# Retention's gate tiles of three heads as block products in the first feed-forward's buffers, with v made one head ahead

## The chip, the core and the metric

The kernel runs on one core of a Trainium2 chip. A core has five engines with queues of their own: TensorE (PE in the profile, its weight loads PEld) multiplies matrices into PSUM; VectorE (DVE), ScalarE (ACT) and GpSimd (POOL) work elementwise; SyncE (SP) mostly issues DMA transfers. Transfers are also issued from ACT's and POOL's queues. The metric is the device time of one launch in microseconds (us), less is better. The kernel before takes 1470.64 us (median of three runs, 1469.88 to 1470.76).

## What is computed

A decoder step of two layers over 544 tokens: 512 of one new sequence, and 32 of eight sample groups of four. All data are float32.

```
x += short_conv(rmsnorm(x));  x += swiglu(rmsnorm(x))        # layer 0
x += retention(rmsnorm(x));   x += swiglu(rmsnorm(x))        # layer 1
return rmsnorm(x), and the new states

retention:  z = x @ w_in                      # (544, 1024) @ (1024, 6144)
            q, k, v, g = split(z)             # 1024, 1024, 2048, 2048 columns; 4 heads
            q, k = rotary(q), rotary(k) / 16
            o = decayed (q k^T) v + q S       # in chunks, per head: dk = 256, dv = 512
            out = (silu(g) * groupnorm(o) * gn_g) @ w_out
swiglu:     (silu(x @ w_gate) * (x @ w_up)) @ w_down        # 2816 hidden
```

The sample groups carry a state S of 256 x 512 for each group and head (1 MB for each of four pieces of a head), which is read, used, updated and written back.

## The kernel before, in words

**Products in two parts.** Every float32 operand is split into a high part (`xh`, `wh`, fp32r) and a low part (`xl`, `wl`), and a product is three: high by high, high by low, low by high. `split` makes the high part with a copy on ACT and the low part with a subtraction on DVE. `split_adding` leaves DVE out: ACT copies twice (the second time negated), and a transfer from POOL's queue adds the original on top. `load_piece` loads a weight piece of 512 KB with SP into one of three buffers `w` of the pool `wts`, and splits it into `wh`, `wl` (three each).

**Tiles.** Activations lie with features on the 128 partitions and the 544 tokens in the free direction, as two halves of 272. `project` multiplies one tile of 128 output features: 8 steps of the contraction x 3 products x 2 halves, 48 products of 272 columns (line 172). PSUM has eight banks: four single ones (`bank`, "sm" in the profile) and two pairs ("mm"), given out by `psum`.

**Feed-forward.** `ffn` takes two output tiles, each cut in two halves of tokens and two of the contraction, as a 2 x 2 block product, and makes it with seven block products in place of eight. `operands` makes the seven combinations of the activation's blocks once (tiles `oh`, `ol`, from a work tile `f` with two buffers); `weights7` makes the seven combinations of a pair of weight tiles. A `Job` is one such pair: 7 block products x 4 steps x 3 = 84 products of 272 columns (line 458). `run` goes through a list of jobs, and prepares the next one's weights while one multiplies. `summed` brings the block products together: snapshots by ACT, additions by DVE, in a tile `gu` (four buffers). The pools of a feed-forward are opened in this order: `ff` (gu), `ffp` (f), `sw` (weights' sums), `ffo` (oh, ol).

**Retention.** After the first feed-forward its pools close and three others open in the same memory: `rt` (most tiles, among them `gt` with the decay tables, `rot0`/`rot1` with the rotated q and k, `gate`, `rt0`, `rt1`, `yn`), `rt1` (small constants and `xs`, the normed sample tokens), `st` (three buffers for pieces of S). `qk_first` makes k and the first half of q for head 0, `qk_project` the other half. Then, for each head:

1. `value`: v for all 512 tokens in four banks (line 906 to 908, 24 products of 512 columns for each of four weight pieces) and for the sample tokens (line 913, which reads the unsplit weights, so `w` stays taken until then). After the second piece come the splits of q and k, the sample scores and the transposed keys.
2. `gate_project` 0, `sample_operands`, `state` 0, `gate_project` 1, `state` 1: two of the head's four gate tiles, and the recurrent state.
3. `scores`, then `gate_project` 2 and 3.
4. `sample_outputs` and `states_update` on the four pieces of S, the outputs `inner`, the normalization, the gating, and in between the next head's k and q (`qk_project`).
5. `out_project`: eight tiles that are added to x.

The last head has gate tiles 2 and 3 inside step 4.

**What sets the order.** The program is written as one list. The framework orders each engine's queue before the run, from a cost estimate of its own: among the instructions whose inputs it reckons ready, the one written first goes first; `issue_after` fixes an order by hand. Waits between engines come from the use of tiles: a tile's buffer is given out again when its last reader is done, and a pool's memory goes to a later pool when the earlier pools in it are closed.

Lines that the change and the steps below speak of:

Of the kernel before, what the change touches and what calls it, by code (L numbers as in the profile page):

```python
# [7 lines left out]
F32 = mybir.dt.float32  # L8
F32R = mybir.dt.float32r
AF = mybir.ActivationFunctionType  # L10
ALU = mybir.AluOpType
# [24 lines left out]
WARM = 8  # L36

# [9 lines left out]
def hybrid_decode_kernel(ctx: ExitStack, tc: tile.TileContext, a: dict, o: dict):  # L47
# [476 lines left out]
    def ffn(layer, next_gain):  # L524
        with ExitStack() as c1:
# [4 lines left out]
            oh = [one.tile([P, 7, HT], F32R, tag=f"oh{i}", name=nm("oh")) for i in range(KP)]  # L530
            ol = [one.tile([P, 7, HT], F32R, tag=f"ol{i}", name=nm("ol")) for i in range(KP)]
# [13 lines left out]

            def operand(k):
                f = fp.tile([P, 5, HT], F32, tag="f", name=nm("f"))
                for i in range(2):
                    nc.vector.scalar_tensor_tensor(
                        f[:, 2 * i : 2 * i + 2, :], halves(x[k + i * KP]), g_ffn(layer, k + i * KP), R,  # L550
                        op0=ALU.mult, op1=ALU.mult,
                    )
                operands(f, oh[k], ol[k])

            def whole_pairs():
# [4 lines left out]
                for m in range(WHOLE):  # L560
# [31 lines left out]
                    for k in range(2 * m, KP if m == WHOLE - 1 else 2 * m + 2):  # L592
                        operand(k)
# [101 lines left out]
            if layer == 1:  # L695
                final(last, group_acts(last), group_weights, fp, tp)

# [83 lines left out]
    ffn(0, lambda kt: g_mix(1, kt))  # L781


    with ExitStack() as c2:
# [23 lines left out]
        for kt in range(KT):  # L808
            nc.vector.tensor_scalar_mul(xs[:, kt, :], x[kt][:, SEQ:], g_mix(1, kt))
# [26 lines left out]
        def qk_first(st):  # L836

            steps = rms_scale(True, [bank(), bank()])
            ws = [load_piece(a["rtqk"][0, 2 + dt], KT * P) for dt in range(2)]
            pts = [psum() for _ in ws]  # L840
            for part in (MADE[:KP], MADE[KP:]):
                for (wh, wl), pt in zip(ws, pts):
                    first = part[0] == MADE[0]
                    project(pt, wh, wl, 0, xh, xl, first, not first, ks=part, weave=iter(()) if first else steps)
            qw, qpt = load_piece(a["rtqk"][0, 0], KT * P), [bank(), bank()]
            project(qpt, *qw, 0, xh, xl, weave=steps)
            drain(steps)
            for i, t in enumerate((cos, sin)):
                nc.sync.dma_start(t, a["rope"][i])
# [21 lines left out]
        def qk_rotate(st, which, dt, pt):  # L871
# [4 lines left out]
            if dt == 0:  # L876
                return
# [484 lines left out]
```

## Time and profile before

| | |
|---|---|
| median of three runs | 1470.64 us (1469.88 to 1470.76) |
| the profiled execution | 1470.36 us, span 1468.5 |
| PE busy | 1457.3 us, 99% |
| DVE, ACT, POOL busy | 920.5, 572.4, 84.3 us |
| moved by DMA | 172.83 MB, mean 118 GB/s |
| granted clock of PE | 0.999 |
| first feed-forward | ends at 574 us on PE |
| retention, head 0's first own product | 574 us |
| retention ends, second feed-forward begins | about 1083 us |
| transfer of a 512 KB weight piece, issue to landing | 3.5 to 4.1 us (median by source) |
| transfer of a 1 MB piece of S, in and out | 7.9 and 4.9 us |

How to read it: a share is of the span. An engine is busy while one of its instructions runs; the DMA share is the mean busy share of 16 DMA engines. "a <- b" in a wait means that a waited until b was done. The chain that ended last is followed back from the last instruction to what released it, step by step.

### The profile page before, as it was taken

How to read it: one execution, taken by the hardware profiler on the slowest of the kernel's cores; microseconds unless marked ns; L12 is line 12 of the kernel's file. 1: busy time of each engine (PE TensorE's matmuls, PEld its weight loads, DVE VectorE, ACT ScalarE, POOL GpSimd, SP SyncE). 2: the span in 40 equal slices, each digit the busy share in tenths (PEclk: the TensorE clock that was granted, in tenths of full speed). 3: DMA queues.
4: the chain of work that ended last, by engine and by line, in shares of the span. 5: the costliest groups of instructions: out<-in, count | busy, mean ns of one | idle time of the engine just before them, and what ended most of it. 6: DMA issues, size and time to landing. Idle time of an engine off the chain costs nothing.

```text
span 1468.5 us, 26015 instructions
## 1 busy us (share of the span) xinstructions
PE 1457.3 (99%) x11016; PEld 1388.8 (95%) x11016; DVE 920.5 (63%) x1397; ACT 572.4 (39%) x821; POOL 84.3 (6%) x107
## 2 busy tenths in 40 slices
PE   9999999999999999999999999999999999999998
PEld 9999999999999999897987988898799999999997
DVE  6545439847748647648645934844759847748645
ACT  5222355625525434242142224114265625525424
POOL 0100220000000003000000000000030000000002
PEclk9999999999999999999999999999999999999999
DMA  6222274232322325336335613714564232332322
GB/s 226 86 87 87 89 179 109 91 100 90 102 94 87 101 65 181 116 115 232 100 115 173 202 49 121 264 42 143 173 158 108 91 105 87 104 92 93 101 65 83
DMA packets 69748, 172.83 MB, mean 118 GB/s; under 512 B 6512, under 2 KB 23792, under 8 KB 69632
## 3 DMA queue, kind: packets, MB, share of 16 engines
q1 hardware_dynamic: 66576, 162.01, 33.9%
q0 software_dynamic: 2192, 7.94, 3.3%
q8 instruction: 86, 1.41, 0.4%
q10 hardware_dynamic: 864, 1.22, 0.2%
q14 instruction: 30, 0.25, 0.1%
HBM read 149.97 MB, written 21.18 MB: 117 GB/s over the span
## 4 chain that ended last, share of the span: by engine, by line
PE 93%; DVE 4%; DMA 2%; POOL 1%; ACT 0%; issue 0%; DVEq 0%; POOLq 0%; ACTq 0%; SPq 0%
PE mm L172 41%; PE sm L458 26%; PE sm L172 13%; PE sm L906 2%; PE sm L907 2%; PE sm L908 2%; DMA S<-in_rets_dram 2%; DVE S L1138 1%; PE sm L160 1%; PE sm L162 1%; PE sm L161 1%; PE sm L1117 1%; PE mm L913 1%; DVE yn L1048 0%; DVE wl L186 0%
## 5 line engine op out<-in xcount | busy, mean ns | idle before, releaser
L185 ACT ACTIVATE wh<-w 128x1024 fp32r<-128x1024 f32 (+4 forms) x215 | 210.0, 980 | 448.2 <-PE mm L172 252.2
L186 DVE TENSOR_TENSOR wl<-w,wh 128x1024 fp32r<-128x1024 f32 (+4 forms) x215 | 243.1, 1134 | 44.3 <-ACT wh L185 40.9
L172 PE MATMUL mm<-xh,wh 128*128 128x272 f32 x1060 | 222.7, 291 | 0.0
L172 PE MATMUL mm<-xh,wl 128*128 128x272 f32 x1060 | 219.2, 289 | 0.0
L172 PE MATMUL mm<-xl,wh 128*128 128x272 f32 x1060 | 218.8, 288 | 0.0
L172 PEld LDWEIGHTS mm<-xh,wh 128*128 128x128 f32 x1060 | 166.5, 189 | 5.0 <-DVE wl L186 3.4
L458 PE MATMUL sm<-oh,wh 128*128 128x272 f32 x576 | 166.7, 289 | 0.0
L458 PE MATMUL sm<-oh,wl 128*128 128x272 f32 x576 | 166.6, 289 | 0.0
L172 PEld LDWEIGHTS mm<-xl,wh 128*128 128x128 f32 x1060 | 166.4, 189 | 0.0
L458 PE MATMUL sm<-ol,wh 128*128 128x272 f32 x576 | 166.3, 289 | 0.0
L172 PEld LDWEIGHTS mm<-xh,wl 128*128 128x128 f32 x1060 | 165.5, 189 | 0.4
L266 DVE TENSOR_TENSOR x<-x,mm 128x544 f32<-128x544 f32 x85 | 61.2, 720 | 144.8 <-PE mm L172 144.8
L458 PE MATMUL sm<-oh,l 128*128 128x272 f32 x432 | 124.9, 289 | 0.0
L458 PE MATMUL sm<-oh,h 128*128 128x272 f32 x432 | 124.8, 289 | 0.0
L458 PE MATMUL sm<-ol,h 128*128 128x272 f32 x432 | 124.8, 289 | 0.0
L458 PEld LDWEIGHTS sm<-oh,wh 128*128 128x128 f32 x576 | 108.7, 189 | 0.5 <-ACT u L515 0.4
L458 PEld LDWEIGHTS sm<-oh,wl 128*128 128x128 f32 x576 | 108.8, 189 | 0.0
L458 PEld LDWEIGHTS sm<-ol,wh 128*128 128x128 f32 x576 | 108.6, 188 | 0.0
L186 DVE TENSOR_TENSOR l<-w,h 128x1024 fp32r<-128x1024 f32 x72 | 68.8, 956 | 55.6 <-ACT h L185 55.4
L172 PE MATMUL mm<-xh,f 128*128 128x272 f32 x576 | 99.3, 288 | 0.0
L172 PE MATMUL sm<-xh,wh 128*128 128x272 f32 x412 | 88.4, 291 | 0.3 <-DVE rs L219 0.3
L172 PE MATMUL sm<-xh,wl 128*128 128x272 f32 x412 | 86.7, 288 | 0.0
(268 smaller groups left out, 2866.5 us busy)
## 6 DMA issues: line engine op xcount, KB each, us to landing
w<-in_ffgu_dram SPq DMA_DIRECT2D x88, 512.0 KB, 3.5
w<-in_ffdn_dram SPq DMA_DIRECT2D x96, 192.0 KB, 2.5
S<-in_rets_dram SPq DMA_DIRECT2D x16, 1024.0 KB, 7.9
out_rets_dram<-S SPq DMA_DIRECT2D x16, 1024.0 KB, 4.9
w<-in_cvin_dram SPq DMA_DIRECT2D x21, 512.0 KB, 3.5
w<-in_rtqk_dram SPq DMA_DIRECT2D x16, 512.0 KB, 3.8
w<-in_rtv_dram SPq DMA_DIRECT2D x16, 512.0 KB, 3.9
w<-in_rtg_dram SPq DMA_DIRECT2D x16, 512.0 KB, 4.1
```

The costliest lines, as they stand in the source:

```text
L160: nc.tensor.matmul(out, lh, rh, start=start, stop=False, skip_group_check=True)
L161: nc.tensor.matmul(out, lh, rl, start=False, stop=False, skip_group_check=True)
L162: last_product[0] = nc.tensor.matmul(out, ll, rh, start=False, stop=stop, skip_group_check=True)
L172: last_product[0] = nc.tensor.matmul(half(pt, hf)[:, :HT], w[:, c], act[k][:, hf * HT : (hf + 1) * HT], start=(first and k == ks[0] and i ...
L185: h = nc.scalar.activation(dh, src, AF.Copy)
L186: nc.vector.tensor_sub(dl, src, dh.bitcast(F32))
L266: last_residual[0] = nc.vector.tensor_add(xk, xk, p)
L458: nc.tensor.matmul(out, w[:, c], b[k][:, at, :], start=(first and k == 0 and i == 0), stop=(k == n - 1 and i == 2), skip_group_check=True,)
L906: nc.tensor.matmul(out, xh[kt][:, ts_], wh[:, cw], start=(kt == 0), stop=False)
L907: nc.tensor.matmul(out, xh[kt][:, ts_], wl[:, cw], start=False, stop=False)
L908: nc.tensor.matmul(out, xl[kt][:, ts_], wh[:, cw], start=False, stop=(kt == KT - 1))
L913: nc.tensor.matmul(pvs[g * NS : (g + 1) * NS, 0, :], xs[:, kt, :], raw[kt // 2][:, kt % 2 * DV : (kt % 2 + 1) * DV], start=(c == 1), stop= ...
```

## The change

The gate tiles of heads 0, 1 and 2 (twelve of sixteen) leave retention. A new function `ahead` runs at the end of the first feed-forward, before its pools close. It makes k, q and v of head 0 and writes them, unrotated, to DRAM; makes the seven operands of the second layer's normed x in the feed-forward's `oh`, `ol`; and runs six jobs, one for each pair of gate tiles, whose results are passed through SiLU, scaled and written to DRAM by transfers from ACT's queue. The last job also loads the first two pieces of head 1's value weights.

Retention then loads: k and q of head 0 (`qk_loaded`, which scales and rotates them), v of the head at hand (`value_loaded`, through the buffer of the `gate` tile), and the finished gate tiles (into that same buffer afterwards). `value` becomes `value_products`, `value_out`, `value_sample` and `operands_made`: in head h the products of head h+1's v run, and its rows go through free buffers to DRAM (`value_out`, stored from ACT's queue). The states' loads are written inside the value products. The last head has no value products any more, and keeps its four gate tiles as they were.

The diff, cut to its core (the products inside `value_products` are those of `value`):

```diff
--- before.py
+++ after.py
+AHEAD = 3
...
+    def operand_tiles(one):
+        return [[one.tile([P, 7, HT], F32R, tag=f"{t}{i}", name=nm(t)) for i in range(KP)] for t in ("oh", "ol")]
+    def operand(k, fp, oh, ol, gain):
+        f = fp.tile([P, 5, HT], F32, tag="f", name=nm("f"))
+        for i in range(2):
+            nc.vector.scalar_tensor_tensor(
+                f[:, 2 * i : 2 * i + 2, :], halves(x[k + i * KP]), gain(k + i * KP), R, op0=ALU.mult, op1=ALU.mult,
+            )
+        operands(f, oh[k], ol[k])
+    def ffn(layer, next_gain, then=None):
...
+            if then is not None:
+                then(tp, fp, sw, one)
...
+    dram = ctx.enter_context(tc.tile_pool(name="dram", bufs=1, space=bass.MemoryType.DRAM))
+    qk_made = [dram.tile([P, 2, T], F32, tag=f"qk{w}", name=nm("qkm")) for w in range(2)]
+    v_made = [dram.tile([P, 5, DV], F32, tag=f"v{h}", name=nm("vm")) for h in range(NH)]
+    gate_made = [dram.tile([P, 4, T], F32, tag=f"g{h}", name=nm("gm")) for h in range(AHEAD)]
+    def value_piece(h, c, raw, adding=False):
+        return load_piece(a["rtv"][h, c], 2 * DV, keep=raw, adding=adding)
+    def value_products(h, xs, first=None, then=None, ws=None):
+        pv = [bank() for _ in range(4)]
+        pvs = psum()
+        if ws is None:
+            raw = []
+            ws = [value_piece(h, c, raw, first is None) for c in range(2)]
+        else:
+            ws, raw = ws
+        if first is not None:
+            first()
+        for c in range(4):
...
+            if c < 2:
+                ws.append(value_piece(h, c + 2, raw, first is None))
+            if then is not None:
+                then(c)
+        return pv, pvs
+    def value_out(h, pv, pvs, places):
+        for tt, (row, _) in enumerate(places):
+            nc.scalar.activation(
+                row, pv[tt] if tt < 4 else pvs[:, 0, :], AF.Copy, scale=rN[:, tt : tt + 1] if tt < 4 else rN[:, 5:6]
+            )
+            if places[tt][1] is not None:
+                at, src = places[tt][1]
+                nc.scalar.dma_start(v_made[h][:, at, :], src)
+    def sample_x(xs):
+        for kt in range(KT):
+            nc.vector.tensor_scalar_mul(xs[:, kt, :], x[kt][:, SEQ:], g_mix(1, kt))
+    def ahead(tp, fp, sw, one):
+        wide("m")
+        steps = rms_scale(True, [bank(), bank()])
+        ws = [load_piece(a["rtqk"][0, 2 + dt], KT * P) for dt in range(2)]
+        pts = [psum() for _ in ws]
+        for part in (MADE[:KP], MADE[KP:]):
+            for (wh, wl), pt in zip(ws, pts):
+                first = part[0] == MADE[0]
+                project(pt, wh, wl, 0, xh, xl, first, not first, ks=part, weave=iter(()) if first else steps)
+        qw, qpt = load_piece(a["rtqk"][0, 0], KT * P, adding=True), [bank(), bank()]
+        project(qpt, *qw, 0, xh, xl, weave=steps)
+        drain(steps)
+        oh, ol = operand_tiles(one)
+        made = [tp.tile([P, 2, T], F32, tag="gu", name=nm("qk")) for _ in range(2)]
+        def off(which, dt, pt):
+            each(lambda p, d, r: nc.vector.tensor_mul(d, p, r), pt, halves(made[which][:, dt, :]), R)
+            if dt:
+                nc.gpsimd.dma_start(qk_made[which], made[which])
+        off(1, 0, pts[0])
+        off(1, 1, pts[1])
+        off(0, 0, qpt)
+        xs = fp.tile([P, KT, NS], F32, tag="f", name=nm("xs"))
+        sample_x(xs)
+        def operand_of(c):
+            operand(c, fp, oh, ol, lambda kt: g_mix(1, kt))
+        pv, pvs = value_products(0, xs, then=operand_of)
+        va = [tp.tile([P, 2, T], F32, tag="gu", name=nm("va")) for _ in range(2)]
+        vs = fp.tile([P, DV], F32, tag="f", name=nm("vs"))
+        rows = [va[tt // 2][:, tt % 2, :DV] for tt in range(4)] + [vs]
+        outs = [None, (slice(0, 2), va[0][:, :, :DV]), None, (slice(2, 4), va[1][:, :, :DV]), (4, vs)]
+        qw = load_piece(a["rtqk"][0, 1], KT * P, adding=True)
+        value_out(0, pv, pvs, list(zip(rows, outs)))
+        qpt = psum()
+        project(qpt, *qw, 0, xh, xl)
+        off(0, 1, qpt)
+        def gates(h, n):
+            made = {}
+            def tile2():
+                if not made:
+                    made[0] = tp.tile([P, 2, T], F32, tag="gu", name=nm("gate"))
+                return made[0]
+            def gate(what, src):
+                g = tile2()
+                if what == "c21":
+                    nc.scalar.activation(g[:, 1, :HT], src, AF.Silu)
+                elif what == "c22":
+                    nc.scalar.activation(g[:, 1, HT:], g[:, 1, HT:], AF.Silu)
+                elif what == "c12":
+                    nc.scalar.activation(g[:, 0, :], g[:, 0, :], AF.Silu)
+                    for i in range(2):
+                        nc.scalar.activation(g[:, i, :], g[:, i, :], AF.Copy, scale=g_ret(h * 4 + n + i))
+                    nc.scalar.dma_start(gate_made[h][:, n : n + 2, :], g)
+            return Job([a["rtg"][h, n + i] for i in range(2)], oh, ol, sw, summed(tile2, gate))
+        def inside(i):
+            if i == 2 * AHEAD - 1:
+                raw = []
+                next_v.extend(([value_piece(1, c, raw) for c in range(2)], raw))
+        run([gates(h, n) for h in range(AHEAD) for n in (0, 2)], inside, lambda i: None)
+    next_v = []
+    ffn(0, lambda kt: g_mix(1, kt), ahead)
...
+        def qk_loaded(st):
             for which in (1, 0):
-                qk_scale(st, which)
-                for dt in range(2 if which else 1):
-                    qk_rotate(st, which, dt, pts[dt] if which else qpt)
+                nc.sync.dma_start(st["rot"][which], qk_made[which])
+                if which:
+                    for i, t in enumerate((cos, sin)):
+                        nc.sync.dma_start(t, a["rope"][i])
+            for which in (1, 0):
+                r = st["rot"][which]
+                nc.vector.tensor_mul(r, r, st["gt"][:, which, :].unsqueeze(1).to_broadcast([P, 2, T]))
+                rotate(st, which)
...
+        def value_loaded(h, st):
+            vw = tp.tile([P, 4, T], F32, tag="gate", name=nm("vw"), bufs=1)[:, :, :DV]
+            vsw = tp.tile([P, DV], F32, tag="yn", name=nm("vsw"))
+            nc.sync.dma_start(vw, v_made[h][:, 0:4, :])
+            nc.sync.dma_start(vsw, v_made[h][:, 4, :])
             vh = tp.tile([P, 4, DV], F32R, tag="vyh", name=nm("vh"), bufs=1)
             vl = tp.tile([P, 4, DV], F32R, tag="vyl", name=nm("vl"), bufs=1)
-            for tt in range(4):
-                nc.scalar.activation(vh[:, tt, :], pv[tt], AF.Copy, scale=rN[:, tt : tt + 1])
-                nc.vector.scalar_tensor_tensor(
-                    vl[:, tt, :], pv[tt], rN[:, tt : tt + 1], vh[:, tt, :].bitcast(F32),
-                    op0=ALU.mult, op1=ALU.subtract,
-                )
-            st["v"] = (vh, vl, v2)
+            for i in range(2):
+                split(vh[:, 2 * i : 2 * i + 2, :], vl[:, 2 * i : 2 * i + 2, :], vw[:, 2 * i : 2 * i + 2, :])
+            st["v"] = [vh, vl, vsw]
+            if h < AHEAD:
+                st["gate"] = tp.tile([P, 4, T], F32, tag="gate", name=nm("gate"), bufs=1)
+                nc.sync.dma_start(st["gate"], gate_made[h])
+        def value_sample(h, st):
+            pt = psum()
+            v4 = tp.tile([P, 2, DV], F32R, tag="rot1", name=nm("v4"), bufs=1)
+            split(v4[:, 0, :], v4[:, 1, :], st["v"][2])
+            for i in range(2):
+                nc.tensor.matmul(pt[:NS, 0, :], sum4, v4[:, i, :], start=(i == 0), stop=(i == 1))
+            v2 = [tp.tile([NS, DV], F32R, tag=f"rt{i}", name=nm("v2"), bufs=1) for i in range(2)]
+            split(*v2, pt[:NS, 0, :])
+            st["v"][2] = v2
+        def operands_made(h, st):
+            qk_split(h, st, 1)
+            qk_split(h, st, 0)
+            sample_scores(h, st)
+            for dt in range(2):
+                qsrc = st["rot"][0][:, dt, SEQ:].rearrange("p (g r s) -> p g r s", g=4, r=2)
+                for r in range(2):
+                    nc.vector.tensor_scalar_mul(
+                        qm[:, dt, :, r, 4 * r : 4 * r + 4], qsrc[:, :, r, :], _gamma(h) ** 4
+                    )
+            keys(h, st)
...
         st = qk_start(0)
-        qk_first(st)
-        qk_project(0, st, 0, 1)
+        qk_loaded(st)
         for h in range(NH):
             more = h + 1 < NH
-            value(h, st)
             st["S"] = {}
-            for i in range(3):
-                states_load(h, st, i)
-            gate_project(h, st, 0)
-            sample_operands(h, st)
-            state(h, st, 0)
-            gate_project(h, st, 1)
-            state(h, st, 1)
+            def first():
+                value_loaded(h, st)
+            def then(c):
+                if c == 0:
+                    for i in range(2):
+                        states_load(h, st, i)
+                elif c == 1:
+                    states_load(h, st, 2)
+                    operands_made(h, st)
+                elif c == 2:
+                    value_sample(h, st)
+            if more:
+                pv, pvs = value_products(h + 1, xs, first, then, None if h else next_v)
+                va = tp.tile([P, 2, DV], F32, tag="rot1", name=nm("va"), bufs=1)
+                vb = [tp.tile([P, DV], F32, tag="yn", name=nm("vb")) for _ in range(2)]
+                sample_operands(h, st)
+                vc = tp.tile([P, DV], F32, tag="rt1", name=nm("vc"), bufs=1)
+                rows = [va[:, 0, :], va[:, 1, :], *vb, vc]
+                outs = [None, (slice(0, 2), va), (2, vb[0]), (3, vb[1]), (4, vc)]
+                value_out(h + 1, pv, pvs, list(zip(rows, outs)))
+                state(h, st, 0)
+                state(h, st, 1)
+            else:
+                gw = load_piece(a["rtg"][h, 0], KT * P)
+                first()
+                for i in range(2):
+                    states_load(h, st, i)
+                operands_made(h, st)
+                gate_project(h, st, 0, ws=gw)
+                value_sample(h, st)
+                states_load(h, st, 2)
+                sample_operands(h, st)
+                state(h, st, 0)
+                gate_project(h, st, 1)
+                state(h, st, 1)
             for c in range(2):
                 scores(h, st, c)
-            if more:
-                gate_project(h, st, 2)
-                gate_project(h, st, 3)
             sample_outputs(h, st, 0)
             states_update(h, st, 0)
             states_load(h, st, 3)
```

## The prediction

> **What bounds the kernel now.** I read the page's busy times, then the chain that ended last, then that chain in order of time, then busy times by stretch.
>
> ```profile
> PE 1457.3 (99%) x11016; PEld 1388.8 (95%) x11016; DVE 920.5 (63%) x1397; ACT 572.4 (39%) x821; POOL 84.3 (6%) x107
> PE 93%; DVE 4%; DMA 2%; POOL 1%; ACT 0%; issue 0%; DVEq 0%; POOLq 0%; ACTq 0%; SPq 0%
> ```
>
> TensorE is idle for 11.2 us of 1468.5, nearly all at the start and the end. So a product taken away is time taken away, if nothing opens a hole; and any hole is loss at once. The two prices of the main edit stand in the chain:
>
> ```profile
> 330.99 63.48 PE sm L458 x504
> ```
> ```profile
> 637.89 5.98 PE mm L172 x48
> ```
>
> 504 block products, which are six jobs, take 63.48 us; one gate tile of 48 products takes 5.98. Now the stretches around the first hand-over to retention and in head 0:
>
> ```profile
> 574.00:600.00 26.00, 26.00 (x212) 26.00 (x211) 17.94 (x36) 7.30 (x9) 2.09 (x4) 1.00 0.67 225
> 649.50:661.30 11.80, 11.80 (x97) 11.80 (x96) 3.50 (x6) 2.99 (x5) 0.00 (x0) 1.00 0.21 65
> 676.00:692.00 16.00, 15.88 (x114) 12.92 (x112) 14.91 (x25) 2.12 (x2) 1.63 (x2) 1.00 0.64 219
> 692.00:708.00 16.00, 15.93 (x129) 15.89 (x129) 15.85 (x26) 6.29 (x8) 0.00 (x0) 1.00 0.91 292
> ```
>
> Columns: length, busy PE, PEld, DVE, ACT, POOL, clock, DMA share, GB/s. TensorE is full in all four. Row 2 is two gate tiles: VectorE works 3.5 of 11.8 us, so these tiles are cover, and cover is what the change takes away. In rows 3 and 4 VectorE is full, but no gate tile lies there. Row 1 is the hand-over: 225 GB/s at a share of 0.67, so about 325 GB/s when all DMA engines are busy (292 at 0.91 gives 321). Last, how a new pool waits for an old one, at the other hand-over (retention to the second feed-forward):
>
> ```profile
> 1081.94 1.37 POOL L215 TENSOR_TENSOR sqacc<-sqacc,sq 128x544 f32<-128x544 f32 x1 [1.22 <-ACT sq L214]
> ```
> ```profile
> 1083.34 0.80 SPq L142 DMA_DIRECT2D w<-in_ffgu_dram  x2
> ```
>
> The load into the new pool's buffer goes out 0.03 us after GpSimd's last read of a square in the old pool (1083.31), though that square lay in another tile. I take it that a pool's memory is handed on when the last use of all the old pool's tiles is over.
>
> **The change, part by part.** The sum is made against the profiled execution, 1470.36 us (span 1468.5 and 1.86 around it), 0.28 below the median 1470.64. Let e be the end of the last gate job's products.
>
> *Gate products.* Twelve tiles leave: 12 x 5.98 = 71.8. Six jobs come: 63.48. Gain 8.3 us, on the path. Ends: 7.5 to 9.0.
>
> *Start of the extra stage.* Operands: four times about 4.9 us of VectorE (two 544-wide products 0.70 each, four 272-wide differences 0.35, low parts 1.50 and 0.65) = 20, plus 6.4 for the first job's weight sums and 3 for taking q and k off PSUM: 29 us, beside the 34.5 us of TensorE from R (about 590.7) through head 0's value products to job 0. But the sample operand holds one of the two f buffers through the value products, so the four operands go one by one, about 8 us each with the two ACT copies (1.35, 0.65): 32 of 34.5. Cover is 2.5 us; I take 0.5, ends 0 and 3. The adding loads cost ACT 6 x 1.06 more, where it is busy 7.3 of 26 us, and POOL 8 issues of 0.87, where it idles 11 us before the power for rN; each lands in 6.4. The nearest, of value piece 0, is ready near 592 and needed at 594.7. Nothing. Moving v, k, q and gates out and back is some 19 MB over 450 us; the stores go by ACT and POOL, 0.35 and 0.87 us an issue, off the path. Nothing, except next.
>
> *Hand-over to retention.* Before, TensorE had k, q and value products to run (574 to 627) while the retention pools filled. Now it has only head 1's value products. The last gate tile ends with an addition 0.43, SiLU 0.66, two copies of 0.75 and some 0.7 of hand-offs, and is then stored from the feed-forward's gu buffer: issue at e+3.3. 256 KB land in 2.9, 1 MB in 4.9; 544 KB beside two state loads take 4. So the pool with gt, rot and vw opens at e+7.3. The state pool lies over the operand buffers and opens at e, so two state loads (2.1 MB) go out first, as a state load before went out at 575.04, as soon as the operands were read. S, S and the store are 2.65 MB = 8.2 us and 2 latency: the rings are free at e+10, gt and k's rot (1.1 MB) have landed at e+13.3. SP's queue behind that: q's rot, v, the sample's v, then value piece 3, which needs a buffer freed at e+12.3 and lands near e+20. VectorE has from e+13.3: 2 x (1.28 + 6 x 0.64) = 10.2 for scaling and rotating; v low parts 2.5; piece 3's low part 1.2; q, k low parts 2.4; sample masks 0.8; key low parts 1.6; v4 0.7: 19.4, to e+32.7; then the sample's sum, two row copies and hand-offs 2.3, and state(0) can have its banks at e+35. Undisturbed it would start at e+27.7 (value products 24.6 with the sample's, transposes and the rest 2.1, placing 1). The hole is 7.3 us. Lower end 0.5 (the chain started at e), upper end 11 (three state loads first, +3.2).
>
> The Trainium skill, in "DMA: Bandwidth & Descriptors", section Anatomy of one DMA, gives for a transfer issued by GpSimd a fixed 2.0 us plus bytes at 436 GB/s. By that the store lands in 3.3 us and k's rot near e+10.8, the hole is 4.8 and the sum 1468.9 (an estimate from that page). The trace has 5.0 us for the 544 KB gt load and 325 GB/s together, so I stay with the rows.
>
> *Heads 1 and 2, and 0 after its state.* The order value, sample operands, state, scores, sample outputs now has no gate tile between. state(1) writes the banks that the mid split reads (0.58 + 0.69 and hand-offs, 1.9 us): the scores' 2.9 us of products can fill that. The score split waits for state(1) (key buffers): 0.53 + 0.56 + 0.3 before inner(0), against 1.7 us of sample outputs and update. Row copies: ACT 5 x 0.69 and four issues of 0.35, partly before the last product. I take 1.0 for the three heads together, ends -1 and 9. SP's order there changes little: v's load falls where the DMA share was 0.13 (708 to 726), the gate load after the v split; value piece 3 waits behind it and still lands in time, as its buffer comes free only after the sample's products.
>
> *Last head.* It keeps its four gate tiles but loses 26 us of value products in front. VectorE has 8.6 us of work in the first 8, but gates 0 and 1 can fill 12 us. 0.5, ends 0 and 3.
>
> **Sum:** 1470.36 - 8.3 + 0.5 + 7.3 + 1.0 + 0.5 = 1471.4. Likeliest: the hole at the hand-over eats the gain. All low ends give 1460.9, all high ends 1488.9.
>
> **Rivals.** *A, the hand-over is covered (faster).* It turns on when VectorE can start: its 19.4 + 2.3 must end by e+27.7, so k's rot must land by e+6. For: the other loads come in time in every hand-over so far (row 1, TensorE 26.00 of 26). Against: the store of the last gate tile alone takes till e+7.3. Hole 1.0: 1465.1.
>
> *B, three state loads go first (slower).* All three buffers of that pool open at e; if the third also goes out before the pool with gt opens, 1.05 MB / 325 = 3.2 us more: hole 10.5, 1474.6. It decides the sign: from a hole of about 9.5 on the change is measurably slower. For: nothing else is ready on SP then. Against: before, SP's order put other loads between the state loads (575.04, 580.55, 586.83).
>
> *C, each head loses 3 us without its gate tiles (slower).* Mid split and score split (1.9 + 1.4) stand bare if state and scores run in written order, since the scores are not put in between. For: nothing else is left to fill with. Against: TensorE's order before already mixes in what is ready. 9 for 1: 1479.4.
>
> **How the numbers follow.** About 0.2% (2.9 us) is what a measurement of this kernel can tell from no change: faster below 1467.7, slower above 1473.6. Forecast 0.40, its own range 1468 to 1475 (0.03 faster, 0.28 same, 0.09 slower); A 0.25 (0.22 faster, 0.03 same); B 0.22 (0.18 slower, 0.04 same); C 0.13, slower. Together 0.25, 0.35, 0.40. The range reaches over A and B and to C's middle: 1463.5 to 1479.5.
>
> **What would show it.** L172 loses 576 products and the jobs gain 504, at 126 ns; the gate groups of heads 0 to 2 are gone from the retention stretch. A hole of TensorE of 5 to 9 us about 20 to 30 us after the last job, ended by VectorE (a rotation, a low part of a value weight or of k), with gt landing near e+12. If gt is issued at e and not 7 us later, A is right. If three state loads stand ahead of gt, B. Idle TensorE of 2 us or more in each head between the value products and the first sample output is C. The prediction is wrong if the hole is under 4 us or if job 0 starts late by more than 3.

## The result, and the profile after

The changed kernel takes 1493.05 us (median of six, 1491.92 to 1497.73) against 1470.78 for the kernel before beside it: ratio 1.0156, interval 1.0141 to 1.017. It is slower by some 22 us, where 1471.4 and at most 1479.5 was forecast. The profiled execution took 1492.83, span 1491.0, 22.5 more than before. Its line numbers differ from those of before: jobs are L460, `project` L174, value products L814 to L816, the sample's value products L821.

Busy times and the chain that ended last, from the page of the changed kernel:

```profile
PE 1458.5 (98%) x10944; PEld 1382.4 (93%) x10944; DVE 960.0 (64%) x1465; ACT 612.1 (41%) x883; POOL 90.8 (6%) x115
PE 88%; DVE 5%; issue 3%; DMA 2%; ACT 1%; POOL 1%; SPq 0%; DVEq 0%; ACTq 0%; POOLq 0%
```

TensorE has 72 products fewer, as it should, but 1.2 us more of busy time, and its idle time went from 11.2 to 32.5 us. So the loss is holes, and products that ran slower. Where they stand is in the waits of TensorE from 590 to 1060 us (total, times, longest):

```profile
PE sm L815 <- DMA wl<-in_rtv_dram: 7.5, 1, 7.5
PE mm L821 <- DMA w<-in_rtv_dram: 4.2, 1, 4.2
PE sm L815 <- DVE wl L188: 2.0, 1, 2.0
PE sm L162 <- ACT vb L835: 1.5, 1, 1.5
PE sm L1233 <- DMA S<-in_rets_dram: 1.4, 1, 1.4
PE sm L162 <- ACT knh L187: 1.3, 2, 0.6
PE mm L951 <- ACT s L187: 1.0, 1, 1.0
```

The first is in the extra stage, the next three at the hand-over to retention, S in head 2, `knh` once at the hand-over and once in the last head, `s` in the last head. The chain in order of time (start, us, what), from the extra stage to head 0's state:

```profile
599.01 15.40 issue
614.43 8.57 DMA wl<-in_rtv_dram
623.04 0.80 PE sm L815
...
635.98 60.52 PE sm L460 x480
...
703.13 13.45 issue
716.77 1.30 DVE rot L980
...
729.28 1.15 DVE wl L188
...
738.03 4.76 DMA vm<-vb
```

480 block products in 60.52 us are 126 ns each: the main edit's price is as forecast. Ahead of them the chain runs through an adding load of v, and behind them through 13.6 us in which VectorE has nothing to work on. The stretches around both holes (length, busy PE, PEld, DVE, ACT, POOL, granted clock, DMA share, GB/s):

```profile
614.00:624.00 10.00, 2.55 (x14) 1.38 (x7) 4.50 (x8) 4.81 (x7) 1.71 (x2) 0.72 0.92 237
624.00:630.00 6.00, 6.00 (x18) 4.70 (x17) 5.96 (x8) 2.42 (x4) 0.00 (x0) 0.62 0.52 123
703.00:717.00 14.00, 14.00 (x65) 10.38 (x64) 0.36 (x2) 0.00 (x0) 0.00 (x0) 1.00 0.81 300
717.00:731.00 14.00, 6.69 (x20) 2.50 (x19) 13.97 (x18) 5.51 (x6) 0.00 (x0) 0.63 0.87 312
```

In row 3 VectorE works 0.36 of 14 us, and in row 4 it is TensorE that has 20 products in 14. Row 2 holds a second surprise: TensorE is busy throughout, with 18 products in 6 us, at a clock of 0.62.

**A ledger by stretch.** I cut each span at five products: the first of head 0's v, the end e of the last gate job, and the first sample output (S times q) of heads 1, 2 and 3. "Due" is what the stretch should take by the trace of before: A = value products 24.6 + a q tile 6.0 + six jobs 63.5; B = 66.9 (594.7 to 661.6) - 6.0 - 23.9 for the gate tiles, + 125.6 - 23.9; C = 126.2 - 23.9; D = 113.5 - 24.6 (v of head 3 is made a head earlier); E is unchanged. In the kernel before, head 0's second q tile starts at 594.7 and v comes behind it; in the changed kernel v comes first, and the q tile counts in A. Last column: time at a granted clock of 0.5 from 560 to 1120 us, added up from windows of 1 us. All are single profiled executions, and stretches of unchanged code differ between them by up to about 1 us ("to v" 594.8 to 596.0). e12_ahead2, with four jobs, is left out.

| kernel | to v | A: to e | B: to head 1 | C: to head 2 | D: to head 3 | E: to end | span | at 0.5 |
|---|---|---|---|---|---|---|---|---|
| due | 594.7 | 94.1 | 138.7 | 102.3 | 88.9 | 441.6 | 1460.2 | 0 |
| changed | 594.8 | 105.4 | 154.2 | 101.3 | 93.3 | 441.9 | 1491.0 | 23.9 |
| e1_piece3 | 595.9 | 99.7 | 153.6 | 101.6 | 94.8 | 441.5 | 1487.2 | 17.1 |
| e2_states | 595.4 | 105.2 | 151.0 | 101.7 | 94.7 | 442.0 | 1490.0 | 20.5 |
| e3_pools | 594.9 | 106.3 | 146.9 | 101.5 | 95.6 | 441.9 | 1487.2 | 17.1 |
| e4_both | 595.0 | 100.1 | 148.4 | 101.4 | 95.6 | 441.6 | 1482.1 | 10.2 |
| e5_both_last | 595.3 | 103.2 | 146.7 | 101.3 | 94.5 | 441.6 | 1482.7 | 10.2 |
| e6_dummies | 595.7 | 111.0 | 153.9 | 101.5 | 95.0 | 441.5 | 1498.6 | 13.7 |
| e7_early | 595.0 | 96.9 | 155.2 | 103.4 | 95.0 | 441.9 | 1487.2 | 13.7 |
| e8_best | 596.0 | 97.5 | 147.5 | 103.1 | 94.6 | 441.7 | 1480.4 | 3.4 |
| e10_two_heads | 595.0 | 97.9 | 145.7 | 101.8 | 92.8 | 441.7 | 1475.0 | 0 |
| e11_dummies40 | 595.2 | 105.6 | 153.9 | 101.6 | 93.5 | 441.4 | 1491.4 | 17.1 |
| e13_last_early | 595.6 | 97.7 | 145.5 | 101.6 | 90.2 | 441.6 | 1472.2 | 0 |

The change earned its 8.3 us and lost 11.3 in A, 15.6 in B and 4.4 in D, with 1.0 back in C: -8.3 + 11.3 + 15.6 - 1.0 + 4.4 + 0.4 = 22.4.

### The profile page after: what moved, and what is told of

Same layout as the page of the kernel before. It is cut to its first block, busy times and chain, and to the rows that moved or that the text cites. A ratio compares the mean times of both kernels' runs of the same rounds, so it can differ in the third digit from the quotient of the medians.

```text
span 1491.0 us, 26121 instructions
## 1 busy us (share of the span) xinstructions
PE 1458.5 (98%) x10944; PEld 1382.4 (93%) x10944; DVE 960.0 (64%) x1465; ACT 612.1 (41%) x883; POOL 90.8 (6%) x115
## 4 chain that ended last, share of the span: by engine, by line
PE 88%; DVE 5%; issue 3%; DMA 2%; ACT 1%; POOL 1%; SPq 0%; DVEq 0%; ACTq 0%; POOLq 0%
PE mm L174 35%; PE sm L460 30%; PE sm L174 12%; PE sm L815 2%; PE sm L816 1%; PE sm L814 1%; PE sm L162 1%; DVE S L1254 1%; PE sm L164 1%; PE sm L163 1%; PE sm L1233 1%; DVE wl L188 1%; DMA S<-in_rets_dram 1%; DMA wl<-in_rtv_dram 1%; DVE xl L200 0%
## 5 line engine op out<-in xcount | busy, mean ns | idle before, releaser
L460 PE MATMUL sm<-oh,wh 128*128 128x272 f32 x672 | 194.3, 289 | 0.0
L460 PE MATMUL sm<-oh,wl 128*128 128x272 f32 x672 | 194.2, 289 | 0.0
L460 PE MATMUL sm<-ol,wh 128*128 128x272 f32 x672 | 193.9, 289 | 0.0
L174 PE MATMUL mm<-xh,wh 128*128 128x272 f32 x868 | 182.3, 291 | 0.5 <-ACT wh L187 0.3
L174 PE MATMUL mm<-xh,wl 128*128 128x272 f32 x868 | 179.5, 289 | 0.0
L174 PE MATMUL mm<-xl,wh 128*128 128x272 f32 x868 | 178.8, 287 | 0.0
L460 PE MATMUL sm<-oh,l 128*128 128x272 f32 x504 | 145.7, 289 | 0.0
L460 PE MATMUL sm<-oh,h 128*128 128x272 f32 x504 | 145.5, 289 | 0.0
L460 PE MATMUL sm<-ol,h 128*128 128x272 f32 x504 | 145.5, 289 | 0.0
L174 PEld LDWEIGHTS mm<-xh,wh 128*128 128x128 f32 x868 | 135.5, 188 | 2.5 <-ACT oh L187 0.8
L174 PEld LDWEIGHTS mm<-xl,wh 128*128 128x128 f32 x868 | 135.9, 188 | 0.1
L174 PEld LDWEIGHTS mm<-xh,wl 128*128 128x128 f32 x868 | 135.3, 188 | 0.6 <-DVE wl L188 0.2
L460 PEld LDWEIGHTS sm<-oh,wh 128*128 128x128 f32 x672 | 126.7, 189 | 0.7 <-ACT u L517 0.4
L460 PEld LDWEIGHTS sm<-oh,wl 128*128 128x128 f32 x672 | 126.8, 189 | 0.0
L460 PEld LDWEIGHTS sm<-ol,wh 128*128 128x128 f32 x672 | 126.6, 188 | 0.0
L174 PE MATMUL mm<-xh,f 128*128 128x272 f32 x576 | 99.3, 288 | 0.0
L460 PEld LDWEIGHTS sm<-ol,h 128*128 128x128 f32 x504 | 95.0, 188 | 0.0
L460 PEld LDWEIGHTS sm<-oh,l 128*128 128x128 f32 x504 | 95.0, 188 | 0.0
```

The source lines that it names most:

```text
L174: last_product[0] = nc.tensor.matmul(half(pt, hf)[:, :HT], w[:, c], act[k][:, hf * HT : (hf + 1) * HT], start=(first and k == ks[0] and i ...
L460: nc.tensor.matmul(out, w[:, c], b[k][:, at, :], start=(first and k == 0 and i == 0), stop=(k == n - 1 and i == 2), skip_group_check=True,)
```

## The experiments

My theory: two loads are late because something keeps their buffers, one in the extra stage and one at the hand-over, and the last head misses the cover it had. The main rival for each: VectorE's own work, or the DMA engines, would hold the stage up wherever the load began.

**e1_piece3: the last adding load taken back.**

```diff
-                ws.append(value_piece(h, c + 2, raw, first is None))
+                ws.append(value_piece(h, c + 2, raw, first is None and c == 0))
```

> One part of the change undone: piece 3 of head 0's value weights is split as in the kernel before (load, low part on VectorE), not by an adding load. Theory (the adding load is late: it needs a buffer that the sample's products free at 607.1, then a load, three ACT copies, an issue and a landing of 8.57 us, so TensorE waits from 612.8 to 623.0): the hole before the c=3 products goes, and with it the low clock behind it. Extra stage 41.0 us from the value products to the first gate job's end of preparation comes back to 30.5 to 32: 9 to 10.5 us off, 1482.5 to 1484. Rival (VectorE or the operands that go one by one through one buffer end last; the hole only moves to the first job): 0 to 3 us off, 1490 to 1493.

1490.52 us, ratio 1.0128 (1.0113 to 1.0143). TensorE's waits from 590 to 640 us:

```profile
PE sm L460 <- ACT wh L187: 1.6, 1, 1.6
PE sm L460 <- ACT h L187: 0.4, 1, 0.4
```

The 7.5 us are gone, and with them the low clock behind them, so the hole needed the adding load; but A fell by 5.7 and not by 9 to 10.5. The first job now waits for its weights: the second of its loads went out at 621.9, when the sample's products had let go of a raw buffer. The time is inside the rival's 1490 to 1493, and the hole did move to the first job in part, though not for the rival's reason (VectorE or the operands): one buffer held two loads, the second hidden behind the first. Of the 5.7, D gave back 1.5, and the stretch ahead of the change another 1.1.

**e3_pools: the store taken off the hand-over's path.** The state pool is opened first, so that `rt` with gt, rot and the values no longer lies over the buffer from which the last gate tile is stored.

```diff
+        sp = c2.enter_context(tc.tile_pool(name="st", bufs=3))
         tp = c2.enter_context(tc.tile_pool(name="rt", bufs=2))
         one = c2.enter_context(tc.tile_pool(name="rt1", bufs=1))
-        sp = c2.enter_context(tc.tile_pool(name="st", bufs=3))
```

> The pool of the state loads is opened before the two pools of gt, rot and the value weights, so that these no longer lie over the buffer from which the last gate tile is stored. Theory (the hand-over's 16 us are that store: issued at e+2.7 behind two state loads, landed at e+10.5, and only then does gt's load go out): gt's load goes out within 1 us of the last job's end e, the first state's product comes at e+37 to e+41 instead of e+53.1: 12 to 16 us off, 1477 to 1481. Rival (VectorE's chain of about 20 us of rotations and low parts is the cause, the store only its start; or the bandwidth of the loads): the loads go out early but land late, and half or less comes back: 1485 to 1489.

**e2_states: head 0's state loads held back behind the other loads.**

```diff
+            st["in"] = nc.sync.dma_start(vsw, v_made[h][:, 4, :])
...
+                if c < 2:
+                    with tc.issue_after(st["in"].ins) if h == 0 else ExitStack():
+                        for i in range(2 * c, 2 + c):
+                            states_load(h, st, i)
```

> The changed kernel with head 0's state loads of the hand-over held back on SyncE's queue until the load of the sample's values has gone out. Theory (the store of the last gate tile lands late, 7.8 us after its issue and not 4, because two state loads of 1 MB went out ahead of it): the store lands 4 to 5 us after its issue, gt's load goes out at e+7 instead of e+10.5, the first sample output at e+48 to e+50 instead of e+53.1: 3 to 6 us off, 1487 to 1490. Rival (the store takes that long by itself, being written to DRAM and waited for, or the state loads are then late for the first sample outputs): 0 to 1 us off, or slower.

e3 took 1489.42 us (1.012, 1.0105 to 1.0135), e2 1492.51 (1.0139, 1.0125 to 1.0153). First the changed kernel, SyncE's queue from 688 us on (start, us, queue, line, what), e being 700.26:

```profile
700.29 0.94 SPq L1223 DMA_DIRECT2D S<-in_rets_dram  x2
710.62 0.34 SPq L964 DMA_DIRECT2D gt<-in_gtab_dram  x1
```

The stores of the last two pairs of gate tiles, from issue to landing, in the changed kernel:

```profile
DMA to landing us min/median/max: 2.7/5.2/7.7
```

The same two stores in e2:

```profile
DMA to landing us min/median/max: 2.7/2.7/2.7
```

SyncE's queue in e2, whose e is 700.56:

```profile
705.92 0.33 SPq L964 DMA_DIRECT2D gt<-in_gtab_dram  x1
```

The store of 544 KB lands in 2.7 us with nothing ahead of it and in 7.7 behind two state loads of 1 MB, and the load of gt goes out at once when it has landed (702.84 + 7.7 = 710.5): at e+10.4 before, at e+5.4 in e2. That the state loads delayed the store is shown, and without them ahead B is 3.2 us shorter. By time little of it arrived: e2 is 0.5 us under the changed kernel, where its rival had 0 to 1 and its theory 3 to 6. In e3 (e = 701.22) the load does not wait for the store at all. SyncE's queue in e3:

```profile
701.25 0.33 SPq L964 DMA_DIRECT2D gt<-in_gtab_dram  x1
```

VectorE's wait for its first rotation in e3, from 700 to 720 us:

```profile
DVE rot L980 <- DMA rot<-qkm: 2.4, 1, 2.4
```

B falls by 7.3, from 15.6 over due to 8.2. So the store is about half of the loss, less than the 12 to 16 expected; the rival's half or less is the nearer, by time too. The expectation looked at the first sample output, which did come at e+38.8 instead of e+52.9, but the order had changed: state products and 1.7 us of waits now follow it, and the way from there to head 1 grew from 101.3 to 108.1. Only the longer stretch is a fair measure. Both kernels lost 1.4 to 2.3 us again in D.

**e4_both, e5_both_last: the two together, and the last head's first gate tile written earlier.** e4 has the edits of e1 and e3; e5 adds:

```diff
-                operands_made(h, st)
                 gate_project(h, st, 0, ws=gw)
+                operands_made(h, st)
```

> Both edits together. If the two holes are separate, the gains add: 21 to 26 us off, 1467 to 1472. If one is hidden behind the other, the sum is less than the two alone by over 3 us. By the sum of the prediction with both holes gone (1470.4 - 8.3 and 1 to 4 in the heads) it would be 1463 to 1466.

> As the one before, and in the last head the first gate tile's products are written ahead of the making of the sample's operands, so that they take the PSUM pair that the sample's scores take otherwise. Theory (the last head loses about 3 us net, since no gate tile can start between value products and state for want of a PSUM pair): 2 to 4 us less than both edits alone: 1463 to 1469. Rival (what is lost in the last head is the value products that went to other heads, not the pair): within 1 us of both edits alone, or slower, as the gate tile then delays the state.

e4: 1485.95 us (1481.04 to 1489.28), ratio 1.01 (1.0072 to 1.0128); e5: 1483.17, 1.0081 (1.0066 to 1.0096). By span each edit alone saves 3.8 us and both together 8.9 (A -5.3, B -5.8), and by medians 2.5 and 3.6 alone and 7.1 together, in a run that spreads over 8 us. So the gains add and the holes are separate; but they are not the 21 to 26 expected. e5's D is 1.1 lower, and its A is 3.1 higher at unchanged code, with 6.8 us at the half clock there: e5 leaves open whether the edit helps.

**e7_early: the sample's products ahead of the value products.** The block that reads the raw weights (L821) is moved ahead of the value products of its chunk; the adding loads stay.

```diff
         for c in range(4):
+            if c % 2:
+                for g in range(4):
...
             wh, wl = ws[c]
```

> The changed kernel with one order altered: the sample's products (from the raw value weights) are written ahead of the value products of the same two chunks, not behind them, so the raw buffers come free about 6 us sooner. The adding loads stay. Theory (in both holes the late load waits for a raw buffer that the sample's products hold): in the extra stage piece 3's load goes out near 601 us and not at 607.2, the hole of 7.5 us shrinks to under 2, and piece 3 at the hand-over is no longer waited for (4.2 us); with the low clock behind both holes 10 to 15 us off, 1478 to 1483. Rival (not the buffer: an adding load's chain of 15 us, ACT, GpSimd and landing, is too long wherever it begins, or the DMA engines are full): 0 to 5 us off, 1488 to 1493.

1490.63 us, 1.0128 (1.0114 to 1.0142). Piece 3's raw load in the changed kernel, from SyncE's queue:

```profile
607.23 0.33 SPq L144 DMA_DIRECT2D w<-in_rtv_dram  x1
```

and the adding transfer that follows from it, from GpSimd's:

```profile
614.43 0.86 POOL L195 DMA_DIRECT2D wl<-in_rtv_dram  x1 [15.42 <-ACT wl L194]
```

The same two in e7, SyncE's first:

```profile
601.83 0.33 SPq L144 DMA_DIRECT2D w<-in_rtv_dram  x1
```

then GpSimd's:

```profile
607.84 0.86 POOL L195 DMA_DIRECT2D wl<-in_rtv_dram  x1 [8.63 <-PE sm L825]
```

With the adding loads kept, A falls by 8.5, more than e1 got by removing the last of them. So the hole took two things, a raw buffer given back at 607 and the long chain of an adding load behind it; taking either away closes it. By time e7 is inside the rival's 1488 to 1493 all the same, as most of the gain went elsewhere: the hand-over still waited 3.6 us for its piece 3 (that load stood in SyncE's queue behind gt's, which waited for the store), C grew by 2.1 and D by 1.7.

**e6_dummies, e11_dummies40: what the low clock costs by itself.** After the value products of chunk 2 (64 products in e6, 40 in e11):

```diff
+            if first is None and c == 2:
+                for _ in range(64):
+                    nc.tensor.matmul(pvs[:, 1, :P], ones, ones, start=True, stop=True, skip_group_check=True)
```

> The changed kernel with 64 products of 128x128 added, whose result nobody reads, in the hole of TensorE before piece 3's products in the extra stage (612.8 to 623.0). Theory (the products behind the hole ran at 0.43 us instead of 0.23 because TensorE had been idle): granted clock 0.95 or more from 618 to 630, where it was 0.53 and 0.62, and 2 to 4 us off: 1489 to 1491. Rival (the low clock came from something else, the load on the DMA engines or a wait that hides between the products): clock and time as before, 1492 to 1494.

> As e6_dummies with 40 added products, whose result nobody reads, instead of 64: those took 14.45 us for a hole of about 9 and so overran it; 40 take 9.0. Theory (the granted clock is halved for whole stretches of 3.41 us, after a stretch in which TensorE was idle): clock 1.00 from 618 to 629, where it was 0.50, the first gate job 2 to 3 us earlier (633 to 634 instead of 635.8), time 2 to 3 us less than the changed kernel if nothing gives it back: 1489 to 1491. Rival (the clock follows something else than idleness): clock 0.50 from 618 to 629, time 1492 to 1494.

e6 took 1500.96 us (1.0198, 1.0182 to 1.0214): 64 products are 14.45 us for a hole of about 9, so it says little of the time. e11 took 1493.21 (1.0151, 1.0136 to 1.0167). The stretch from 619 to 628 us in the changed kernel, with the clock third from the end:

```profile
619.00:628.00 9.00, 4.96 (x12) 3.89 (x13) 5.08 (x7) 2.78 (x3) 0.00 (x0) 0.50 0.79 207
```

and in e11:

```profile
619.00:628.00 9.00, 9.00 (x58) 7.64 (x61) 3.19 (x4) 3.37 (x5) 0.00 (x0) 1.00 0.45 85
```

The clock follows idleness: with the hole filled it stays at 1.00, and piece 3's value products, 0.43 us apart before, came every 0.23. The time did not follow: the first job came at 634.9, 0.9 us earlier and not 2 to 3, and the median is the changed kernel's. The sample's products, which had run inside the hole, now came behind the filling (628.9 instead of 614.9), so the raw buffer went back 14 us later, and the jobs' next weights with it: the jobs took 65.9 us instead of 64.4, and A stayed at 105.6.

**e8_best, e10_two_heads, e13_last_early: the causes together.** e8 is e4 with the sample's products first; e10 has these first only for the values of heads 0 and 1, and e5's order in the last head; e13 also moves the last head's operands into the output products of head 2:

```diff
+                if n2 == 1 and mid:
+                    wide("m")
+                    mid()
+                    wide("mms")
...
-                out_project(h, st)
+                out_project(h, st, mid=None if h + 2 < NH else lambda: operands_made(h + 1, nxt))
...
-                operands_made(h, st)
                 gate_project(h, st, 0, ws=gw)
```

> Plain split of piece 3, the pools in the other order and the sample's products first, together. e4_both still waits 3.1 us for piece 3 at the hand-over and 1.8 us for the first job's weights, whose second load waits for a raw buffer until 621.0; both buffers now come free about 6 us sooner. Theory: 5 to 8 us less than e4_both, 1477 to 1481: still slower than before by what the last head and the shorter waits cost. If it comes out under 1471, the three causes are all there was; if at 1484 or more, the raw buffers were not what held these loads.

> As e8_best, but the sample's products come first only in the extra stage and at the hand-over (values of heads 0 and 1), since in e8_best heads 1 and 2 took 103 us from one first sample output to the next where all others took 101.4; and with the last head's first gate tile ahead of the sample's operands, as in e5_both_last. Theory (the earlier order costs 1.7 us in each of the later heads and saves only where a load is late): 3 to 5 us less than e8_best, 1478 to 1480. Rival (heads 1 and 2 were longer because head 0 began earlier, work only moved): as e8_best, 1482 to 1484.

> As e10_two_heads, and the last head's operands (low parts of q and k, sample scores, transposed keys) are made in the middle of head 2's output products instead of at the head of the last head. Theory (the last head loses because that chain between TensorE, VectorE and ScalarE lies bare there: waits of 0.57, 1.00 and 0.62 us in one stretch and the halved clock behind them, 3.4 to 6.8 us long): no wait over 0.3 us and no halved clock at the start of the last head, 3 to 5 us less than e10_two_heads, 1474 to 1477. Rival (that work then delays the output products, or the gate tiles wait for PSUM pairs): within 1.5 us of e10_two_heads, or slower.

e8: 1483.0 us (1.0076, 1.0063 to 1.0089), within e4's spread and short of the 5 to 8 us expected; e10: 1476.95 (1.0041, 1.0028 to 1.0055), better than expected; e13: 1475.79 (1.003, 1.0021 to 1.0039), inside the 1474 to 1477 expected, though only 1.2 below e10 by medians (2.8 by span), not the 3 to 5 expected but within the 1.5 of its rival. e10's C is back from 103.1 to 101.8 and its B from 147.5 to 145.7, so the earlier order did cost heads 1 and 2. In the profiled executions of e10 and e13 no microsecond from 560 to 1120 is below full clock. e13's longest waits from 590 to 1060 us (its lines are 5 further on here):

```profile
PE sm L460 <- DVE wl L188: 1.7, 1, 1.7
PE mm L811 <- DMA w<-in_rtv_dram: 1.7, 1, 1.7
PE sm L1238 <- DMA S<-in_rets_dram: 1.0, 2, 0.7
```

Nothing of the last head is left among them, and D is down to 90.2, so the bare chain of the sample's scores and keys was one part of what D had lost. The other was not in the last head: D also holds head 2's wait for a piece of S, 1.4 us in the changed kernel, 1.7 in e10 and 0.7 in e13, which is 1.0 of the 2.6 us between these two. e13 recovers 17 of the 22 us and is still 4.6 us slower than the kernel before: by the ledger 3.6 remain in A and 6.8 in B, against a gain of 8.3. TensorE's waits make 2.0 and 3.7 us of these; the rest was not traced. No version here beats the kernel before.

**e12_ahead2: one size changed.** `AHEAD = 2`, and head 2 makes its own gate tiles where the kernel before makes them.

> Two heads' gate tiles ahead instead of three: four jobs, and head 2 makes its own four gate tiles, at the places in its order where the kernel before makes them. Theory (jobs gain 2.77 us a head and a head without gate tiles loses nothing; the losses stand in the extra stage, the hand-over and the last head): 2.0 to 3.5 us more than the changed kernel, 1495 to 1497. Rival (each head without gate tiles loses about 3 us for want of cover, or head 2 without them spoils the start of the last head): 0 to 4 us less than the changed kernel, 1489 to 1493.

1497.15 us (1.0177, 1.0163 to 1.0191), 4.1 more than the changed kernel: a little over the 2.0 to 3.5 expected, with 27.3 us at the half clock where the changed kernel has 23.9, and on the other side of the rival. A head that gives its gate tiles away gains; it does not lose 3 us for want of them. The ledger says the same: C is 1.0 under due in the changed kernel, and in e12, where head 2 keeps its tiles, it is 125.5 against 126.2.

## Why the prediction was wrong

*Gate products, -8.3:* right (126 ns a product; the jobs' stretch took 64.4 with its waits).

*Start of the extra stage, 0.5 (0 to 3):* the first step that failed; it took 10.4 more than due, and the jobs 0.9. The text's own mark, job 0 late by more than 3, was passed. The failing sentence is "The nearest, of value piece 0, is ready near 592 and needed at 594.7. Nothing." Piece 0 was the wrong one to look at. Piece 3 needs a buffer that the sample's products of pieces 0 and 1 give back at 607, and from there load, copies, issue and landing take 15.8 us to 623.0, while TensorE needs it at 612.8. The buffer rule stood in my own text, where piece 3 at the hand-over "needs a buffer freed at e+12.3"; I did not apply it one stage earlier. The other half of the step, operands one by one through f, did not end last.

*Hand-over to retention, 7.3 (0.5 to 11):* the mechanism was right (a pool opens when the last store is over, two state loads go out first), the sizes were not; the stretch lost 15.6. The store went out at e+2.6, not e+3.3, but landed after 7.7 us, not 4.0: I added the bytes of all three transfers for the loads behind them and not for the store itself. VectorE began at e+16.5 instead of e+13.3. Piece 3's raw load, behind gt's on SyncE's queue, landed at e+22.3 and not near e+20, and TensorE waited 4.2 us for it, its longest wait there. I let the hole end when VectorE's last step was done; in fact piece 3's low part (e+30.2) still had value products behind it, at half the clock, so that the state began at e+39.2 instead of e+35. And a wait that I had not named followed: a row of head 1's v waits for `yn`, whose two buffers hold the sample's v and another row not yet stored (4.76 us in the chain, 1.5 on TensorE).

By the Trainium skill ("DMA: Bandwidth & Descriptors", Anatomy of one DMA), the store would land in 3.3 us, an estimate from its fit for transfers that GpSimd issues, while this store went from ACT's queue. The trace has 2.7 with nothing ahead, so for a lone transfer that was nearer than my 4.0; the 2 MB ahead, which neither figure counts in full, decided.

*Heads 1 and 2, and 0 after its state, 1.0 (-1 to 9):* head 2 gave -1.0 (C). Head 1, from the first sample output of head 0 to its own, took 101.3 against 125.6 - 23.9 = 101.7, so -0.4. Head 0's share lies in B and can't be told apart. Heads 1 and 2 together are at or just under the lower end; rival C is refuted, by these and by e12.

*Last head, 0.5 (0 to 3):* 4.4, of which 1.4 is head 2's wait for a piece of S and 2.2 are three waits at the start of the last head (0.57, 1.00, 0.62). I counted VectorE's 8.6 us against gate tiles that "can fill 12 us", but the first of them starts at 1028.1, behind the sample's scores and the keys. Written ahead of these (e10) it brought D from 93.3 to 92.8; moving the chain itself under the output products (e13) brought 90.2, 1.0 of it from the shorter wait for S.

*Rivals:* A needed gt's load at e; it went out at e+10.4. B needed three state loads first; two did. What came, two loads ahead that make the store itself late, was none of mine. The range took each bound from one stretch, and even all high ends together, 1488.9, lie under the measured time; besides piece 3 they lacked that a hole also slows what comes after it.

## What to carry to other kernels

When a load is said to be hidden, ask it of the last load of the stage and not of the first, and date it from the moment its buffer comes free: here the reader of the raw weights, not the load, set the time. When a pool is handed on through a store, what went out on other queues just before it lengthens it (here 7.7 us instead of 2.7). A gain won in one stretch should be looked for at the end of the kernel: of 8.5 us saved in e7's extra stage and jobs, 3.8 arrived.

## What the runs showed of the hardware

**Half a clock, in steps of 3.4 us.** Windows of 1 us show, but for those at the edges, a granted clock of either 1.00 or 0.50, and the low times last 3.4, 6.8, 10.2 or 13.7 us. From 560 to 1120 us the kernel before has none and the changed kernel has 23.9 us of it, behind both holes (every kernel has some at the very end of its span, the kernel before 3.7 us). Long holes are not needed. In the last head three short waits (0.57, 1.00, 0.62 us), the same in all kernels with its old order, left the clock alone in the changed kernel and halved it for 6.8 us in e4. The changed kernel there:

```profile
1020.00:1030.00 10.00, 7.80 (x58) 6.71 (x57) 6.63 (x9) 5.07 (x8) 0.00 (x0) 1.00 0.25 91
```

and e4:

```profile
1010.00:1020.00 10.00, 7.80 (x37) 6.22 (x36) 6.63 (x9) 5.07 (x8) 0.00 (x0) 0.70 0.18 52
```

Both have 7.80 us of TensorE at work, but 58 products in the one and 37 in the other. The price is regular. From the first of the three waits to the last head's first sample output, at the same code, it is 26.4 us in the changed kernel without half clock, 27.9 with 3.4 us of it (e1, e2, e6, e7, e8, e11, e12) and 29.4 with 6.8 (e3, e4): 1.5 us for each step of 3.4 us. That is what e1, e2, e3 and e7 gave back in D, but for some tenths of the wait for S, and it comes and goes with the moment at which the waits fall.

The Trainium skill ("TensorE: Matmul & The Clock Gate", What's actually happening) says that the clock has two states, full and half, set by how busy TensorE was in a free-running window of 3.41 us. The steps measured here agree. The same section of the Trainium skill lets the clock fall after an idle window of about 3.4 us; in the last head waits of at most 1.00 us were enough, so the measurement goes further. That the windows run free would explain why equal waits cost differently, and the spread of e4's and e13's times (8 and 6 us), but no run here shows the windows themselves.

**A small store behind large loads.** 2.7 us alone, 7.7 behind 2 MB issued 2.5 us earlier on another queue. It landed 0.1 us after the second of these loads, which itself took 9.7 us, so both were late. Smaller neighbours count too: the four earlier stores of gate tiles, each issued 0.15 us after a weight load of 512 KB, took 5.6 to 6.1 us in the changed kernel.
